# A chunked state-space scan: the old state's product scaled after the matmul, and three elementwise steps moved to GpSimd

## The chip, the core and the metric

The kernel runs on one core of one Trainium2 chip. The metric is the device time of one execution in microseconds (us). A core has five engines that run beside each other: PE (TensorE, matrix products into PSUM), DVE (VectorE), ACT (ScalarE), POOL (GpSimd) and SP (SyncE, which here issues all DMAs). Each takes its instructions in a fixed order that is settled when the program is built; they wait for each other by semaphores.

## The reference

One block of 2048 tokens by 1024 channels goes through a Mamba-2 layer, then through an attention layer with a sliding window. The change lies in the scan of the Mamba-2 layer, in chunks of 128 tokens, with 4 groups of 8 heads of 64 channels and a state of 128 per head. Cut to that:

```python
a_cum = jnp.cumsum(dt * a.reshape(SSM_GROUPS, SSM_HPG), axis=2)
xdt = x * dt[..., None]
seg = a_cum[:, :, :, None] - a_cum[:, :, None, :]
decay = jnp.exp(jnp.where(causal, seg, -jnp.inf))
cb = jnp.einsum('bcign,bcjgn->bcijg', cm, bm)
y_diag = jnp.einsum('bcijg,bcijgr,bcjgrp->bcigrp', cb, decay, xdt)
decay_to_end = jnp.exp(a_cum[:, :, -1:] - a_cum)
states = jnp.einsum('bcjgn,bcjgr,bcjgrp->bcgrpn', bm, decay_to_end, xdt)
chunk_decay = jnp.exp(a_cum[:, :, -1])
...
    return carry * dec[..., None, None] + st, carry
...
y_off = jnp.einsum('bcign,bcgrpn,bcigr->bcigrp', cm, prev, jnp.exp(a_cum))
return (y_diag + y_off).reshape(b, s, SSM_HEADS, SSM_HEAD_DIM)
...
y = y + d_skip.astype(jnp.float32)[:, None] * xs.astype(jnp.float32)
```

After it y is gated by SiLU(z), normed over each group and projected back.

## The kernel before

The tokens are cut into 4 blocks of 512, each block into 4 groups of channels: 16 units. For unit n the kernel computes ten products of the block's input with weight tiles (`gemm_steps`, L444 on): six go through a causal convolution (`conv`: B, C and four tiles of x), four become the gate (`zz`). One such product is 24 PE instructions at L163 into a PSUM tile `g` (two of them exist). The weights come by DMA (`ws`), ACT makes a rounded copy and DVE the remainder (L112, L113), two products ahead of their use.

While unit n's products run, the scan of unit n-1 runs beside them (`ssd_steps`). The list `SSD` gives the order of its steps, which are laid between the products' steps; on top of that the compiler's scheduler orders each engine's instructions. A unit has 4 chunks c, each with two halves hf of 4 heads:

- `l` (`load`, L547): a DMA broadcasts a row of the cumulated decays (`acd`) to `ab`, one per half.
- `p` (`prep`, L526): PE transposes x to `xt` and B to `bc`, and multiplies B by C; DVE makes `xdt` (L538) and `xw` (L540), `cbm` (L544).
- `h` (`half`, L552): ACT makes `ea` = exp(ab) (L557) and `seg` (L561, L562), DVE multiplies `ea` by C (L563) and `seg` by `cbm` (L564).
- `r` (`prod`, L567): PE adds in `y` the chunk's own part (L576, from `seg`) and the old state's part (L580: weights `prev`, moving `ea`).
- `f` (`fin`, L582): PE makes the chunk's own state `st` (L587), DVE multiplies the state `prev` by the chunk's decay (L589) and adds `st` (L590); DVE adds the skip term to y (four L593, into `yt`) and gates (two L597); ACT squares into `q` (L598); POOL adds the squares into `gacc` (L599, L602).
- `s` (`gn_sum`): PE transposes `gacc` to `rb` (L98), from which the group's norm comes.

In three units (the third group of blocks 0 to 2) the input norm of the next block is taken as well: ACT squares eight tiles (`sq`, L281), POOL adds them into `sqa` (L282). The convolution keeps its three last columns in `carry`, copied by POOL (L468, L474).

All of this is f32. `xt`, `bc`, `y`, `st` and `g` lie in PSUM, the other tiles named here in SBUF. PSUM is full: `y`, `xt`, `bc`, `st` one bank each, two for `rb` and two for `g`. The tail of the program, from about 1300 us, is the attention layer; the change leaves the order of its instructions as it is.

Of the kernel before, what the change touches and what calls it, by code (L numbers as in the profile page):

```python
# [9 lines left out]
F32 = mybir.dt.float32  # L10
F32R = mybir.dt.float32r
I32 = mybir.dt.int32
AF = mybir.ActivationFunctionType
ALU = mybir.AluOpType
# [43 lines left out]
def trunk(ctx: ExitStack, tc: tile.TileContext, xT, pT, pos, wts, wdt, vec, out):  # L58
    nc = tc.nc
# [12 lines left out]
    def vc(name, i=0, n=1):  # L72
        o = _V[name][0] + i
        return VA[0][:, o : o + n] if o < NVA else V[:, o - NVA : o - NVA + n]
# [226 lines left out]
    with ExitStack() as sa:  # L301
        sp = sa.enter_context(tc.tile_pool(name="sa", bufs=2))
        one = sa.enter_context(tc.tile_pool(name="oa", bufs=1))
        tp = sa.enter_context(tc.tile_pool(name="ta", bufs=2))
        pa = sa.enter_context(tc.tile_pool(name="paa", bufs=1, space=PSUM))
# [29 lines left out]
        prev = one.tile([128, 4, 512], F32, name="prev")  # L335
# [62 lines left out]
        def dt_path(b, ps):  # L398
# [12 lines left out]
            t = lambda n: one.tile([128, 128], F32, tag=n, name=n)  # L411
# [23 lines left out]
            wend = one.tile([128, 128], F32, tag="wend", name=f"wend{b}", bufs=2)  # L435
            nc.vector.tensor_tensor(wend, pm[:, 128:256], ac, op=ALU.subtract)
            nc.scalar.activation(wend, wend, AF.Exp)
            nc.vector.tensor_tensor(wend, wend, dt, op=ALU.mult)
            cdec = one.tile([128, 128], F32, tag="cdec", name=f"cdec{b}", bufs=2)
            nc.scalar.activation(cdec, pm[:, 128:256], AF.Exp)  # L440
            at = one.tile([128, 128], F32, tag="at", name="at")
# [80 lines left out]
        def ssd_steps(n):  # L522
# [3 lines left out]
            st8 = {}  # L526

            def prep(c):
                cs = slice(c * 128, c * 128 + 128)
                col = slice(c * 32 + 8 * g, c * 32 + 8 * g + 8)  # L530
                xt = pa.tile([128, 8, 64], F32, tag="xt", name="xt")
                for t in range(4):
                    nc.tensor.transpose(xt[:, 2 * t : 2 * t + 2].rearrange("p a b -> p (a b)"), xbc[t // 2][:, t % 2, cs], ident)
                bc = pa.tile([128, 256], F32, tag="bc", name="bc")
                nc.tensor.transpose(bc[:, 0:128], xbc[2][:, 0, cs], ident)
                nc.tensor.matmul(bc[:, 128:256], xbc[2][:, 0, cs], xbc[2][:, 1, cs], start=True, stop=True)
                xdt = sp.tile([128, 8, 64], F32, tag="xdt", name="xdt")
                nc.vector.tensor_tensor(xdt, xt, dt[:, col].unsqueeze(2).broadcast_to((128, 8, 64)), op=ALU.mult)  # L538
                xw = sp.tile([128, 8, 64], F32, tag="xw", name="xw")
                nc.vector.tensor_tensor(xw, xt, wend[:, col].unsqueeze(2).broadcast_to((128, 8, 64)), op=ALU.mult)  # L540
                bt = sp.tile([128, 128], F32, tag="bt", name="bt")
                nc.scalar.copy(bt, bc[:, 0:128])
                cbm = sp.tile([128, 128], F32, tag="cbm", name="cbm")
                nc.vector.tensor_tensor(cbm, bc[:, 128:256], tri, op=ALU.mult)  # L544
                st8[c] = [xdt, xw, bt, cbm, None]

            def load(c, hf):  # L547
                ab = st8["ab", c, hf] = sp.tile([128, 4, 128], F32, tag="ab", name="ab")
                i = 8 * c + 2 * g + hf
                nc.sync.dma_start(ab.rearrange("p a b -> p (a b)"), acd[i : i + 1, :].broadcast_to((128, 512)))  # L550

            def half(c, hf):  # L552
                cs = slice(c * 128, c * 128 + 128)
                cbm = st8[c][3]
                ab = st8.pop(("ab", c, hf))
                ea = sp.tile([128, 4, 128], F32, tag="ea", name="ea")
                nc.scalar.activation(ea, ab, AF.Exp)  # L557
                seg = sp.tile([128, 4, 128], F32, tag="seg", name="seg")
                for h in range(4):
                    hc = c * 32 + 8 * g + 4 * hf + h  # L560
                    nc.scalar.activation(seg[:, h], ab[:, h], AF.Relu, scale=-1.0, bias=ac[:, hc : hc + 1])  # L561
                nc.scalar.activation(seg, seg, AF.Exp, scale=-1.0)  # L562
                nc.vector.tensor_tensor(ea, ea, xbc[2][:, 1, cs].unsqueeze(1).broadcast_to((128, 4, 128)), op=ALU.mult)  # L563
                nc.vector.tensor_tensor(seg, seg, cbm.unsqueeze(1).broadcast_to((128, 4, 128)), op=ALU.mult)  # L564
                st8[c, hf] = (ea, seg)

            def prod(c, hf):  # L567
                if hf == 0:
                    st8[c][4] = pa.tile([128, 4, 128], F32, tag="y", name="y")
                xdt, y = st8[c][0], st8[c][4]  # L570
                ea, seg = st8.pop((c, hf))
                for t in range(2):
                    for r in range(2):
                        h = 4 * hf + 2 * t + r
                        o = y[64 * r : 64 * r + 64, 2 * hf + t, :]
                        nc.tensor.matmul(o, xdt[:, h], seg[:, 2 * t + r], start=True, stop=False)  # L576
                    for r in range(2):
                        h = 4 * hf + 2 * t + r
                        o = y[64 * r : 64 * r + 64, 2 * hf + t, :]
                        nc.tensor.matmul(o, prev[:, g, 64 * h : 64 * h + 64], ea[:, 2 * t + r], start=False, stop=True)  # L580

            def fin(c):  # L582
                cs = slice(c * 128, c * 128 + 128)
                col = slice(c * 32 + 8 * g, c * 32 + 8 * g + 8)
                xdt, xw, bt, cbm, y = st8.pop(c)
                st = pa.tile([128, 512], F32, tag="st", name="st")
                nc.tensor.matmul(st, bt, xw.rearrange("p a b -> p (a b)"), start=True, stop=True)  # L587
                pv = prev[:, g].rearrange("p (a b) -> p a b", a=8)
                nc.vector.tensor_tensor(pv, pv, cdec[:, col].unsqueeze(2).broadcast_to((128, 8, 64)), op=ALU.mult)  # L589
                nc.vector.tensor_tensor(prev[:, g], st, prev[:, g], op=ALU.add)  # L590
                yt = sp.tile([128, 4, 128], F32, tag="yt", name="yt", bufs=1)
                for t in range(4):
                    nc.vector.scalar_tensor_tensor(yt[:, t], xbc[t // 2][:, t % 2, cs], vc("dsk", 4 * g + t), y[:, t],  # L593
                                                   op0=ALU.mult, op1=ALU.add)
                q = sp.tile([128, 4, 128], F32, tag="q", name="q", bufs=1)
                for t in range(2):
                    nc.vector.tensor_tensor(sz[t][:, :, cs], yt[:, 2 * t : 2 * t + 2], sz[t][:, :, cs], op=ALU.mult)  # L597
                    nc.scalar.activation(q[:, 2 * t : 2 * t + 2], sz[t][:, :, cs], AF.Square)  # L598
                nc.gpsimd.tensor_tensor(q[:, 0:2], q[:, 0:2], q[:, 2:4], op=ALU.add)  # L599
                if c == 0:  # L600
                    st8["acc"] = tp.tile([128, T], F32, tag="gacc", name="gacc", bufs=1)
                nc.gpsimd.tensor_tensor(st8["acc"][:, cs], q[:, 0], q[:, 1], op=ALU.add)  # L602
# [535 lines left out]
```

## Time and profile before

| | us |
|---|---|
| median of 3 runs | 2926.93 (2926.82 to 2929.85) |
| the profiled execution | 2929.66 |
| its span, first to last instruction | 2927.8 |
| PE busy | 2883.9 (98%) |
| DVE busy | 2242.7 (77%) |
| ACT busy | 1633.8 (56%) |
| POOL busy | 379.9 (13%) |
| DMA, mean busy share of 16 engines | 34% |

How to read it. Busy time is the union of an engine's instructions; PE's ends are modelled, so a busy PE need not be at its peak. PEld is PE's loading of weights, which overlaps its products. The table by stretches gives for each stretch its length, then busy us (and number of instructions) of PE, PEld, DVE, ACT and POOL, then the granted clock as a share of 2.4 GHz, the DMA share and GB/s. The list of waits gives who waited for whom: us in total, times, the longest. Groups of instructions read: line, engine, operation, out<-in, shapes, count | busy us, mean ns of one | idle time of the engine before them and who ended it. For one line or tile: the count, then the shortest, median and longest in ns, then the first and last start in us. In a timeline each row is: start us, us, engine, line, operation, out<-in, shapes, how many in a row, and in brackets the idle time before and what ended it. DMA issues give the count, KB each and the median us to landing. L12 is line 12 of the kernel of before.

### The profile page before, as it was taken

The page shows a single profiled execution, that of the slowest core. Times are in us where ns is not written, and L with a number is a line of the kernel's source. Part 1 is how long each engine was busy: PE and PEld are TensorE (multiplying, and loading weights), DVE is VectorE, ACT ScalarE, POOL GpSimd, SP SyncE. Part 2 cuts the span into 40 slices and gives each one's busy share as a digit, 9 for nine tenths or more (in the row PEclk, how much of TensorE's full clock was granted, in tenths as well). Part 3 has the DMA queues.
Part 4 walks back from the last instruction along what each step waited for, and adds up shares of the span by engine and source line. Part 5 has one row for each costly group of instructions (what it writes and reads, how often), then busy time and mean ns, then how long its engine had stood idle before and what let it go on. Part 6 is the DMA issues. An engine that isn't in the chain of part 4 may idle for free.

```text
span 2927.8 us, 41254 instructions
## 1 busy us (share of the span) xinstructions
PE 2883.9 (98%) x14648; PEld 2250.0 (77%) x14648; DVE 2242.7 (77%) x4919; ACT 1633.8 (56%) x3309; POOL 379.9 (13%) x439
## 2 busy tenths in 40 slices
PE   8999999999999999999999999999999999999999
PEld 6777777777777777778777888777888768887667
DVE  7999989998899888766786646876556876557864
ACT  5666666666666666544665334674335764345752
POOL 1121113111311111111001011001010001010001
PEclk9999999999999999999999999999999999999999
DMA  4433433343333333533123532124422124432112
GB/s 161 137 109 117 137 120 107 114 138 126 105 119 113 116 119 121 172 110 95 59 74 113 176 95 90 54 97 134 147 94 83 57 94 138 144 94 89 51 62 82
DMA packets 134125, 319.43 MB, mean 109 GB/s; under 512 B 21152, under 2 KB 46624, under 8 KB 132896
## 3 DMA queue, kind: packets, MB, share of 16 engines
q1 hardware_dynamic: 133920, 316.80, 33.5%
q8 instruction: 115, 1.88, 0.3%
q14 instruction: 90, 0.74, 0.1%
HBM read 290.80 MB, written 25.95 MB: 108 GB/s over the span
## 4 chain that ended last, share of the span: by engine, by line
PE 50%; DVE 2%; ACT 1%; DMA 1%; issue 0%; SPq 0%; POOL 0%; ACTq 0%; POOLq 0%
PE g L163 12%; PE o L163 8%; PE tk L787 7%; PE gt L163 6%; PE ao L163 6%; PE pv L867 4%; PE pp L163 3%; PE pt L863 2%; PE sc L830 1%; PE sc L831 1%; PE qtp L979 1%; DMA raw<-ydr 0%; PE ktp L956 0%; DMA ws<-in_wts 0%; DVE w L146 0%; ACT P L847 0%
## 5 line engine op out<-in xcount | busy, mean ns | idle before, releaser
L163 PE MATMUL g<-u,w 128*128 128x512 f32 x5136 | 1239.4, 395 | 1.2 <-DVE x L492 0.7
L163 PEld LDWEIGHTS g<-u,w 128*128 128x128 f32 x5136 | 953.3, 188 | 220.2 <-issue 21.6
L112 ACT ACTIVATE w<-ws 128x1024 fp32r<-128x1024 f32 x336 | 355.3, 1058 | 410.1 <-PE g L163 137.9
L113 DVE TENSOR_TENSOR w<-ws,w 128x1024 fp32r<-128x1024 f32 x336 | 418.5, 1246 | 93.4 <-ACT w L112 92.8
L282 POOL TENSOR_TENSOR sqa<-sqa,sq 128x512 f32<-128x512 f32 x105 | 161.0, 1533 | 1482.2 <-ACT sq L281 1481.3
L163 PE MATMUL o<-y,w 128*128 128x512 f32 x1248 | 295.9, 392 | 4.1 <-ACT y L112 4.1
L787 PE MATMUL tk<-w,u 128*128 128x512 f32 x1152 | 291.2, 397 | 0.0
L163 PEld LDWEIGHTS o<-y,w 128*128 128x128 f32 x1248 | 232.9, 188 | 57.3 <-ACT y L112 6.8
L787 PEld LDWEIGHTS tk<-w,u 128*128 128x128 f32 x1152 | 210.4, 188 | 42.2 <-issue 3.2
L479 DVE SCALAR_TENSOR_TENSOR acc<-raw,cw,acc 128x512 f32<-128x512 f32 x288 | 219.9, 765 | 4.6 <-ACT acc L477 4.6
L163 PE MATMUL ao<-o,w 128*128 128x512 f32 x768 | 195.0, 397 | 2.5 <-DVE h L991 2.5
L163 PE MATMUL gt<-u,w 128*128 128x512 f32 x768 | 184.1, 394 | 4.3 <-ACT hsq L797 4.3
L561 ACT ACTIVATE seg<-ab,ac 128x128 f32<-128x128 f32 x512 | 166.6, 392 | 24.0 <-PE y L576 24.0
L145 ACT ACTIVATE w<-ws,V 128x256 fp32r<-128x256 f32 (+1 forms) x224 | 123.2, 597 | 93.9 <-issue 33.0
L146 DVE SCALAR_TENSOR_TENSOR w<-ws,V,w 128x256 fp32r<-128x256 f32 (+1 forms) x224 | 126.5, 595 | 63.0 <-ACT w L145 62.4
L163 PEld LDWEIGHTS gt<-u,w 128*128 128x128 f32 x768 | 141.3, 188 | 34.4 <-ACT hsq L797 6.0
L847 ACT ACTIVATE P<-P,nm,r 128x256 f32<-128x256 f32 x256 | 150.7, 591 | 28.9 <-DVE nm L841 28.9
L163 PEld LDWEIGHTS ao<-o,w 128*128 128x128 f32 x768 | 139.5, 188 | 33.8 <-issue 9.4
L599 POOL TENSOR_TENSOR q<-q 128x256 f32<-128x256 f32 x64 | 77.4, 1210 | 372.0 <-ACT q L598 372.0
L473 ACT COPY raw<-g 128x512 f32<-128x512 f32 x90 | 52.6, 585 | 127.6 <-PE g L163 126.5
L481 ACT ACTIVATE th<-acc 128x512 f32<-128x512 f32 x96 | 60.5, 631 | 101.7 <-DVE acc L479 101.7
L867 PE MATMUL pv<-pt,VV 128*64 128x512 f32 x256 | 113.9, 618 | 0.7
(231 smaller groups left out, 4352.9 us busy)
## 6 DMA issues: line engine op xcount, KB each, us to landing
ws<-in_wts SPq DMA_DIRECT2D x368, 512.0 KB, 3.5
ab<-acd SPq DMA_DIRECT2D x128, 256.0 KB, 3.4
ws<-in_wts SPq DMA_DIRECT2D x96, 256.0 KB, 2.9
ydr<-x SPq DMA_DIRECT2D x32, 512.0 KB, 2.6
raw<-ydr SPq DMA_DIRECT2D x48, 256.0 KB, 4.3
x<-in_xT SPq DMA_DIRECT2D x32, 256.0 KB, 5.2
h<-in_xT SPq DMA_DIRECT2D x8, 1024.0 KB, 6.0
out_h<-h SPq DMA_DIRECT2D x32, 256.0 KB, 2.8
```

The costliest lines, as they stand in the source:

```text
L112: nc.scalar.activation(hi, src, AF.Copy)
L113: nc.vector.tensor_tensor(lo, src, hi.bitcast(F32), op=ALU.subtract)
L145: nc.scalar.activation(w[:, 0, sl], raw[:, sl], AF.Copy, scale=sc)
L146: nc.vector.scalar_tensor_tensor(w[:, 1, sl], raw[:, sl], sc, w[:, 0, sl].bitcast(F32), op0=ALU.mult, op1=ALU.subtract)
L163: nc.tensor.matmul(ps, w[:, p, kw, cols], act[ka][:, q], start=first and j == 0 and r == 0, stop=last and j == n - 1 and r == 2)
L282: self.eng.tensor_tensor(self.acc, self.acc, q, op=ALU.add)
L479: nc.vector.scalar_tensor_tensor(acc, raw[:, j : j + T], tap(j), acc, op0=ALU.mult, op1=ALU.add)
L561: nc.scalar.activation(seg[:, h], ab[:, h], AF.Relu, scale=-1.0, bias=ac[:, hc : hc + 1])
L599: nc.gpsimd.tensor_tensor(q[:, 0:2], q[:, 0:2], q[:, 2:4], op=ALU.add)
L787: nc.tensor.matmul(res[s], a[k][:, x, s * 128 : s * 128 + 128], w[:, y, k % 2], start=k == 0 and j == 0, stop=k == 7 and j == 2)
L847: nc.scalar.activation(P[:, h], P[:, h], AF.Exp, scale=r8[:, h : h + 1], bias=nm[:, h : h + 1], accum_out=den[:, h : h + 1])
L867: nc.tensor.matmul(pv[64 * r : 64 * r + 64, :], VV[:, s + kh, 64 * a : 64 * a + 64], pts[r][:, kh], start=kh == 0, stop=kh == 1)
```

## The change

The old state's part of y is no longer made from `ea` times C. PE multiplies `prev` by C directly, for all 8 heads in four products of 128 weight columns, into a PSUM tile `off` (which shares its bank with `st`); DVE multiplies `off` by exp(a_cum), which a DMA now lays out by channel in a tile `ea` of its own; POOL adds the result to `yt`. POOL also does `xw` (now from `xdt`), the skip products (into `yt`, already in `prep`) and the state's decay. DVE then adds y to `yt` in one instruction. The core of the diff:

```diff
-            nc.vector.tensor_tensor(wend, wend, dt, op=ALU.mult)
...
-                nc.vector.tensor_tensor(xw, xt, wend[:, col].unsqueeze(2).broadcast_to((128, 8, 64)), op=ALU.mult)
+                nc.gpsimd.tensor_tensor(xw, xdt, wend[:, col].unsqueeze(2).broadcast_to((128, 8, 64)), op=ALU.mult)
...
+                yt = sp.tile([128, 4, 128], F32, tag="yt", name="yt")
+                for t in range(2):
+                    nc.gpsimd.tensor_tensor(yt[:, 2 * t : 2 * t + 2], xbc[t][:, :, cs],
+                                            vc("dsk", 4 * g + 2 * t, 2).unsqueeze(2).broadcast_to((128, 2, 128)), op=ALU.mult)
...
+                if hf == 0:
+
+                    ea = st8["ea", c] = sp.tile([128, 4, 128], F32, tag="ea", name="ea")
+                    rows = acd.rearrange("a (t r i) -> (a t) r i", t=2, r=2)
+                    for r in range(2):
+                        nc.sync.dma_start(ea[64 * r : 64 * r + 64],
+                                          rows[2 * i : 2 * i + 4, r].unsqueeze(0).broadcast_to((64, 4, 128)))
...
-                ea = sp.tile([128, 4, 128], F32, tag="ea", name="ea")
-                nc.scalar.activation(ea, ab, AF.Exp)
+                if hf == 0:
+                    nc.scalar.activation(st8["ea", c], st8["ea", c], AF.Exp)
...
-                nc.vector.tensor_tensor(ea, ea, xbc[2][:, 1, cs].unsqueeze(1).broadcast_to((128, 4, 128)), op=ALU.mult)
...
+                    off, ea, yt = pa.tile([128, 4, 128], F32, tag="st", name="off"), st8.pop(("ea", c)), st8[c][5]
+                    for t in range(4):
+                        nc.tensor.matmul(off[:, t], prev[:, g, 128 * t : 128 * t + 128], xbc[2][:, 1, cs], start=True, stop=True)
+                    nc.vector.tensor_tensor(ea, off, ea, op=ALU.mult)
+                    nc.gpsimd.tensor_tensor(yt, yt, ea, op=ALU.add)
...
-                        nc.tensor.matmul(o, xdt[:, h], seg[:, 2 * t + r], start=True, stop=False)
-                    for r in range(2):
-                        h = 4 * hf + 2 * t + r
-                        o = y[64 * r : 64 * r + 64, 2 * hf + t, :]
-                        nc.tensor.matmul(o, prev[:, g, 64 * h : 64 * h + 64], ea[:, 2 * t + r], start=False, stop=True)
+                        nc.tensor.matmul(o, xdt[:, h], seg[:, 2 * t + r], start=True, stop=True)
...
-                nc.vector.tensor_tensor(pv, pv, cdec[:, col].unsqueeze(2).broadcast_to((128, 8, 64)), op=ALU.mult)
+                nc.gpsimd.tensor_tensor(pv, pv, cdec[:, col].unsqueeze(2).broadcast_to((128, 8, 64)), op=ALU.mult)
...
-                yt = sp.tile([128, 4, 128], F32, tag="yt", name="yt", bufs=1)
-                for t in range(4):
-                    nc.vector.scalar_tensor_tensor(yt[:, t], xbc[t // 2][:, t % 2, cs], vc("dsk", 4 * g + t), y[:, t],
-                                                   op0=ALU.mult, op1=ALU.add)
+                nc.vector.tensor_tensor(yt, yt, y, op=ALU.add)
```

The change also moves instructions on the engines. In the changed kernel `xw` is L539, the skip products L546, `ea`'s DMAs L559, its exp L567, `off` L586, off times ea L587, the yt add L588, y's own part L593, `st` L600, the state's decay L602, its sum L603, yt plus y L604, the gating L607, ACT's squares L608, q and gacc L609 and L612; the other lines differ from before by one to ten.

POOL in a unit with the next block's norm, before: the carry copies, the sums of the squares (`sqa`) and of the gated output (`q`, `gacc`).

```order
L474 COPY carry<-raw 128x3
L468 COPY raw<-carry 128x3
L282 TENSOR_TENSOR sqa<-sqa,sq 128x512 x2
L599 TENSOR_TENSOR q<-q 128x256
L602 TENSOR_TENSOR gacc<-q 128x128
L282 TENSOR_TENSOR sqa<-sqa,sq 128x512 x4
L474 COPY carry<-raw 128x3
L282 TENSOR_TENSOR sqa<-sqa,sq 128x512
```

The same place in the changed kernel, from the state's decay of the unit's second chunk on:

```order
L602 TENSOR_TENSOR prev<-prev,cdec_2971 128x512
L467 COPY raw<-carry 128x3
L546 TENSOR_TENSOR yt<-x_0_3669,VA 128x256
L546 TENSOR_TENSOR yt<-x_1_3670,VA 128x256
L539 TENSOR_TENSOR xw<-xdt,wend_2968 128x512
L609 TENSOR_TENSOR q<-q 128x256
L282 TENSOR_TENSOR sqa<-sqa,sq 128x512
L612 TENSOR_TENSOR gacc<-q 128x128
L282 TENSOR_TENSOR sqa<-sqa,sq 128x512 x2
L588 TENSOR_TENSOR yt<-yt,ea 128x512
L282 TENSOR_TENSOR sqa<-sqa,sq 128x512 x4
L473 COPY carry<-raw 128x3
```

Ahead of the series stand four of the moved instructions and within it a fifth; the carry copy now comes after the last sum.

ACT at that place, before: the squares for the norm (`sq`) and for the output (`q`), and the copy of a product's PSUM tile `g` to `raw`, after which L477 frees it.

```order
L281 ACTIVATE sq<-x_4751 128x512 x2
L598 ACTIVATE q<-x_3_3738 128x256
L598 ACTIVATE q<-x_4_3739 128x256
L281 ACTIVATE sq<-x_4751 128x512 x2
L557 ACTIVATE ea<-ab 128x512
L281 ACTIVATE sq<-x_4751 128x512 x2
L473 COPY raw<-g 128x512
L281 ACTIVATE sq<-x_4751 128x512
L477 ACTIVATE acc<-g,cw 128x512
```

And in the changed kernel:

```order
L608 ACTIVATE q<-x_4_3673 128x256
L281 ACTIVATE sq<-x_4672 128x512 x2
L571 ACTIVATE seg<-ab,ac_2966 128x128
L281 ACTIVATE sq<-x_4672 128x512 x2
L571 ACTIVATE seg<-ab,ac_2966 128x128
L281 ACTIVATE sq<-x_4672 128x512
L571 ACTIVATE seg<-ab,ac_2966 128x128
L281 ACTIVATE sq<-x_4672 128x512 x2
L472 COPY raw<-g 128x512
L476 ACTIVATE acc<-g,cw 128x512
```

The copy moved from ahead of the last square to behind it, and parts of the next `seg` stand between the squares.

DVE at the end of an ordinary unit, before: the last chunk's state, skip term and gating, up to the reduction of `rb` (L100), which follows PE's transposes of `gacc`.

```order
L492 SCALAR_TENSOR_TENSOR x_4_3739<-th,g 128x512
L113 TENSOR_TENSOR w_4397<-ws_4395,w_4397 128x1024
L589 TENSOR_TENSOR prev<-prev,cdec_3021 128x512
L593 SCALAR_TENSOR_TENSOR yt<-x_0_2957,VA,y 128x128
L590 TENSOR_TENSOR prev<-st,prev 128x512
L593 SCALAR_TENSOR_TENSOR yt<-x_0_2957,VA,y 128x128
L593 SCALAR_TENSOR_TENSOR yt<-x_1_2958,VA,y 128x128 x2
L597 TENSOR_TENSOR x_3_2960<-yt,x_3_2960 128x2x128
L597 TENSOR_TENSOR x_4_2961<-yt,x_4_2961 128x2x128
```

And in the changed kernel:

```order
L491 SCALAR_TENSOR_TENSOR x_4_4370<-th,g 128x512
L587 TENSOR_TENSOR ea<-off,ea 128x512
L113 TENSOR_TENSOR w_5044<-ws_5042,w_5044 128x1024
L603 TENSOR_TENSOR prev<-st,prev 128x512
L604 TENSOR_TENSOR yt<-yt,y 128x512
L607 TENSOR_TENSOR x_3_3672<-yt,x_3_3672 128x2x128
L607 TENSOR_TENSOR x_4_3673<-yt,x_4_3673 128x2x128
L100 TENSOR_REDUCE rmsx<-rb 128x4
```

Five instructions left this stretch of DVE and two came; between off times ea (L587) and yt plus y (L604) lies POOL's yt add, during which DVE has a weight remainder (L113).

## Rows read from the trace of the kernel before

**Rows 1.** Busy times by stretches, the scan's stretch.

```profile
100.00:1240.00 1140.00, 1128.68 (x6460) 884.13 (x6459) 1025.43 (x1913) 720.17 (x1490) 231.08 (x318) 1.00 0.37 122
```

**Rows 2.** Waits of PE over the whole run.

```profile
PE y L576 <- DVE seg L564: 4.3, 3, 1.4
PE rb L98 <- POOL gacc L602: 4.2, 6, 1.0
```

**Rows 3.** Timeline of PE, from 240 to 242 us.

```profile
240.40 0.39 PE L536 MATMUL bc<-x 128*128 128x128 f32 x2
240.62 0.60 PE L98 MATMUL rb<-ident,sqa 128*128 128x128 f32 x4
...
241.42 0.39 PE L580 MATMUL y<-ea,prev 128*64 128x128 f32 x4
241.64 0.39 PE L576 MATMUL y<-seg,xdt 128*64 128x128 f32 x4
```

**Rows 4.** Groups of instructions, DVE and ACT, whole run.

```profile
L563 DVE TENSOR_TENSOR ea<-ea,x 128x512 f32<-128x512 f32 x128 | 90.4, 714 | 0.0
...
L557 ACT ACTIVATE ea<-ab 128x512 f32<-128x512 f32 x128 | 79.7, 623 | 3.9 <-DMA ab<-acd 2.9 <-PE y L580 0.5 <-DMA ydr<-x 0.4
...
L593 DVE SCALAR_TENSOR_TENSOR yt<-x,VA,y 128x128 f32<-128x128 f32 x256 | 77.2, 340 | 0.0
...
L589 DVE TENSOR_TENSOR prev<-prev,cdec 128x512 f32<-128x512 f32 x64 | 48.8, 763 | 6.0 <-PE y L580 5.3
...
L590 DVE TENSOR_TENSOR prev<-st,prev 128x512 f32<-128x512 f32 x64 | 43.7, 682 | 0.2 <-issue 0.2
...
L540 DVE TENSOR_TENSOR xw<-xt,wend 128x512 f32<-128x512 f32 x64 | 43.5, 680 | 0.0
```

**Rows 5.** POOL's instructions at L282 and at L599: shortest, median, longest.

```profile
L282 POOL TENSOR_TENSOR sqa<-sqa,sq x105: 1271/1362/2159, 184.8 to 2868.7; 128x512 f32<-128x512 f32 x105
...
L599 POOL TENSOR_TENSOR q<-q x64: 726/936/2308, 114.8 to 1270.3; 128x256 f32<-128x256 f32 x64
```

**Rows 6.** DVE's instructions at L597, L593 and L113: shortest, median, longest.

```profile
L597 DVE TENSOR_TENSOR x<-yt,x x128: 407/418/1518, 113.5 to 1269.3; 128x256 f32<-128x256 f32 x128
...
L593 DVE SCALAR_TENSOR_TENSOR yt<-x,VA,y x256: 329/340/348, 111.0 to 1268.7; 128x128 f32<-128x128 f32 x128
...
L113 DVE TENSOR_TENSOR w<-ws,w x336: 1195/1221/2285, 11.1 to 2902.7; 128x1024 fp32r<-128x1024 f32 x168
```

**Rows 7.** Busy times by stretches, a series of sqa.

```profile
184.80:197.40 12.60, 11.17 (x69) 8.48 (x69) 11.71 (x12) 6.43 (x13) 11.39 (x9) 1.00 0.13 43
```

**Rows 8.** Timeline of all engines in that stretch.

```profile
184.84 2.95 DVE L597 TENSOR_TENSOR x<-yt,x 128x256 f32<-128x256 f32 x2
...
190.57 2.29 DVE L113 TENSOR_TENSOR w<-ws,w 128x1024 fp32r<-128x1024 f32 x1
...
190.79 0.44 PE L576 MATMUL y<-seg,xdt 128*64 128x128 f32 x4 [1.43 <-DVE seg L564]
...
191.80 0.63 ACT L281 ACTIVATE sq<-x 128x512 f32<-128x512 f32 x1 [2.00 <-POOL sqa L282]
...
191.82 5.74 PE L163 MATMUL g<-u,w 128*128 128x512 f32 x24
192.78 1.77 DVE L563 TENSOR_TENSOR ea<-ea,x 128x512 f32<-128x512 f32 x1
...
194.48 1.78 DVE L589 TENSOR_TENSOR prev<-prev,cdec 128x512 f32<-128x512 f32 x1
```

**Rows 9.** Groups of POOL between 100 and 1240 us.

```profile
L282 POOL TENSOR_TENSOR sqa<-sqa,sq 128x512 f32<-128x512 f32 x21 | 33.1, 1576 | 3.8 <-ACT sq L281 2.9
```

**Rows 10.** Timeline at the end of an ordinary unit.

```profile
450.38 0.47 POOL L602 TENSOR_TENSOR gacc<-q 128x128 f32<-128x128 f32 x1
...
450.94 0.60 PE L98 MATMUL rb<-ident,gacc 128*128 128x128 f32 x4
```

**Rows 11.** DMA issues: the row of ab.

```profile
ab<-acd SPq DMA_DIRECT2D x128, 256.0 KB, 3.4
```

More of the change, by code (lines that the diff above doesn't have):

```diff
@@ L544, in prep @@
                 nc.vector.tensor_tensor(cbm, bc[:, 128:256], tri, op=ALU.mult)
-                st8[c] = [xdt, xw, bt, cbm, None]
+                yt = sp.tile([128, 4, 128], F32, tag="yt", name="yt")
+                for t in range(2):
+                    nc.gpsimd.tensor_tensor(yt[:, 2 * t : 2 * t + 2], xbc[t][:, :, cs],
+                                            vc("dsk", 4 * g + 2 * t, 2).unsqueeze(2).broadcast_to((128, 2, 128)), op=ALU.mult)
+                st8[c] = [xdt, xw, bt, cbm, None, yt]
             def load(c, hf):
@@ L562, in half @@
                 nc.scalar.activation(seg, seg, AF.Exp, scale=-1.0)
-                nc.vector.tensor_tensor(ea, ea, xbc[2][:, 1, cs].unsqueeze(1).broadcast_to((128, 4, 128)), op=ALU.mult)
                 nc.vector.tensor_tensor(seg, seg, cbm.unsqueeze(1).broadcast_to((128, 4, 128)), op=ALU.mult)
-                st8[c, hf] = (ea, seg)
+                st8[c, hf] = seg
             def prod(c, hf):
@@ L570, in prod @@
                 xdt, y = st8[c][0], st8[c][4]
-                ea, seg = st8.pop((c, hf))
+                seg = st8.pop((c, hf))
+                if hf == 0:
+                    cs = slice(c * 128, c * 128 + 128)
+                    off, ea, yt = pa.tile([128, 4, 128], F32, tag="st", name="off"), st8.pop(("ea", c)), st8[c][5]
[3 more added lines that the diff above has]
+                    nc.gpsimd.tensor_tensor(yt, yt, ea, op=ALU.add)
                 for t in range(2):
@@ L584, in fin @@
                 col = slice(c * 32 + 8 * g, c * 32 + 8 * g + 8)
-                xdt, xw, bt, cbm, y = st8.pop(c)
+                xdt, xw, bt, cbm, y, yt = st8.pop(c)
                 st = pa.tile([128, 512], F32, tag="st", name="st")
```

## The prediction

> **What bounds the kernel now.** I read the busy times of the scan's stretch first, then the waits of PE, then lines and single instructions. Between 100 and 1240 us PE is busy 1128.7 of 1140 us, at a granted clock of 1.00, its 2.4 GHz level [rows 1]. So at most 11.3 us of PE's idle time can be won there, 0.4% of the run, unless PE's own work gets shorter. DVE is second with 1025.4 us (90%), POOL has 231 us [rows 1]. What PE waits for by name is small: 4.3 us for seg from DVE and 4.2 us for gacc from POOL, over the whole run [rows 2]. The reader is to see that DVE at 90% sits beside a PE at 99%: work taken from DVE is taken from an engine on which PE hardly waits.
>
> **PE.** The 512 products of prev with ea (1024 instructions of 64 weight columns) become 256 products off with 128 columns (512 instructions). They look halved, but are not: two 64-column instructions run side by side on the two halves of the array. Four L580 start at 241.42 and the next four instructions at 241.64, 55 ns each; two full-width L536 start at 240.40 and the next at 240.62, 110 ns each [rows 3]. So 1024 x 0.055 = 56 us go and 512 x 0.110 = 56 us come. Below, nothing lets off run faster than L536. Above, 10% for eight full-width weight loads in a row, an estimate: 6 us more. I take +1 us.
>
> **DVE and ACT.** Gone from DVE: ea times C 90.4, xw 43.5, the state's decay 48.8, the skip term 77.2 us: 259.9 us [rows 4]. New on DVE: off times ea and yt plus y, 64 each. Both have one input in PSUM, as L590 has, 683 ns [rows 4]: 87.4 us. Net 172.5 us off DVE. ACT loses half of L557, 39.9 us [rows 4]; it waits on others most of the time there (720 of 1140 us busy [rows 1]), so I cost it at nothing; its cover is the PE products it runs beside.
>
> **POOL.** It gains five instructions in each of 64 chunks: xw, the state's decay and yt plus ea at 512 columns, two skip products at 256. The nearest rows are sqa, 1.27 us at best, and q, 0.73 at best [rows 5]: 64 x (3 x 1.27 + 2 x 0.73) = 337 us. With its 231 us that is about half of the stretch. POOL is not full, but its work runs into DVE's. When POOL works, a DVE instruction with both inputs in SBUF stretches: L597 goes from 418 to 1518 ns and L113 from 1221 to 2285, while L593, with an input in PSUM, never exceeds 348 [rows 6]. POOL stretches too: q from 0.73 to 2.31 us [rows 5].
>
> How much DVE loses is the disputed price. One stretch shows it: from 184.8 to 197.4 us POOL is busy 11.39 us [rows 7]. There two L597 take 2.95 instead of 0.84 us; L113 takes 2.29 instead of 1.22; L563 takes 1.77 and L589 1.78, where their groups average 0.71 and 0.76 [rows 4, 6, 8]. That is 2.1 + 1.1 + 1.1 + 1.0 = 5.3 us, 0.47 us of DVE for each us of POOL. The 337 us would then cost DVE 158 us: of the 172.5 us taken off it, 14 stay off. The lower end is none lost, since a POOL instruction can fall into DVE's idle time; the upper end is all 337. I take 0.47, the row in which POOL runs as densely as it now will. DVE stays near 90%.
>
> The Trainium skill ("SBUF — State Buffer", Who interferes with whom) states the stronger rule: a DVE instruction with two SBUF inputs and a GpSimd instruction that reads SBUF exclude each other for the whole instruction, and the second fully blocks. By it the sum would take the upper end, the second rival; the stretch above shows half of that.
>
> **What becomes late.** In PE's order the next chunk's off mostly comes 5 us or more behind st, so the decay on POOL (which waits only for off of its own chunk) has room, and xw is wanted some 20 us after it can start (estimates from the pitch of single instructions [rows 3, 8]). Two places have no room.
>
> First, the three units in which the next block's norm is summed (sqa). POOL's order there puts a decay, two skip products, xw and a yt add into the series of squares, and ACT's copy of a gemm's PSUM tile now stands behind all squares, where before it stood ahead of the last. ACT already stood still 2.0 us there for one sqa [rows 8]. From off of the second chunk to the square that frees the copy POOL does eight 512-column instructions at the stage's mean of 1.58 us [rows 9], three of 256 at 0.94 (q's median [rows 5]), gacc 0.47 [rows 10] and a small copy 0.2: 16.1 us. Three ACT instructions of 0.62 (L557's mean [rows 4]) follow: 18.0. PE comes back for that bank after 23 gemm instructions, a half y, st, 24 gemm instructions, xt and bc. A gemm's 24 take 5.6 us (5.74 with the last one's end [rows 8]), the small ones about 2.1 us at 0.11 us per 128 columns [rows 3]: 13.1 us. PE waits 4.9 us, three times: +14.7 us. The 1.43 us that it waits for seg at this spot in each of the three units [rows 2, 8] are swallowed: -4.3 us. Between none (POOL finds the gaps) and 9 us per unit, this term is the widest.
>
> Second, each unit's end. The last gacc ends 0.1 us before PE starts the transposes on it: 450.38 + 0.47 against 450.94 [rows 10]. Now the chain is off, decay and yt add on POOL, yt plus y and the gating on DVE, ACT, q, gacc. Four L593 and the decay leave DVE there (1.4 and 0.8 us [rows 4]); yt plus y (0.7) and the yt add (1.27) enter, so the bare chain is as long as before, 2.0 against 2.2. But the add now meets DVE's L113 (1.22 us [rows 6]) on the way; I count a third of it, 0.4, less the 0.2: 0.2 us later in each of 15 units, +3 us, between -4.2 (all of PE's wait gone [rows 2]) and +15 (the whole L113 each time, less the 0.2).
>
> **SP and the queues.** 128 more DMAs, each half of ab, which lands in 3.4 us [rows 11]. They are issued one or two chunks ahead, but wait for POOL to free ea; the weight loads queue behind them on SP. A gemm's weights are split two gemms ahead, some 11 us, so this is covered unless POOL falls behind by more than that.
>
> Sum: +1 + 14.7 - 4.3 + 3 = +14.4 us on the profiled execution's 2929.7, 2944.1. That execution lies 2.7 above the median of the runs, 2926.9, so the time to compare is 2941.4 us, 0.5% slower.
>
> **Rivals.** (a) Faster. DVE is relieved after all, because POOL's instructions fall into DVE's idle time and its PSUM inputs; the waits at both places stay as they are and PE's idle time in the stretch goes: at best 2926.9 - 11.3 = 2916, likelier 2919 (both named waits gone, 8.5 us [rows 2]). For it: 115 us of the stretch have DVE idle [rows 1]. Against: all that PE could win is 11 us, and POOL now stands in two chains that it did not stand in. It decides if DVE loses under 0.2 us per us of POOL.
> (b) The port fills. By the rule above each us of POOL costs DVE one: 1025 - 172 + 337 = 1190 us of DVE in a stretch of 1140, 50 us too much: 2977. For it: L597 at 1518 ns waited for nearly a whole sqa [rows 6]. Against: 0.47 in the one dense stretch. It decides from about 0.85 us per us.
> (c) No change: POOL keeps up in the three units, PE's waits trade places, within 6 us of 2927.
>
> **How the numbers follow.** About 0.2%, 5.9 us, is what a measurement of this kernel can tell from no change. Chances: forecast (2931 to 2955) 0.46, (a) 0.17, (b) and what lies toward it 0.14, (c) 0.23. The lower end of the range is (a)'s likelier value, 2919, the upper (b)'s, 2977; some 2 in 10 lie outside. Faster 0.17 is (a). Slower is (b) and the forecast less its near edge, 0.55. The rest, 0.28, is no change.
>
> **What would show it.** Right: between 100 and 1240 us PE's off group takes as long as y from ea did; POOL is busy about 600 us or more; DVE stays above 85%, with L113, L478 and L573 stretched; PE waits some us for ACT's copy in the three units with sqa. Wrong: DVE below 80% busy with its two-input instructions near their medians (rival a); DVE at 98% and PE waiting for seg and weights in every unit (rival b); off groups at another pitch than 0.11 us; PE waits in units without sqa.

## The result and the profile after

The changed kernel takes 3023.4 us (median of 4 runs, 3020.2 to 3026.4) against 2928.0 for the kernel before: a ratio of 1.032, 95% interval 1.031 to 1.033. It is slower by 95 us, where 14 were forecast and 50 were the worst that the range allowed for. The profiled execution has a span of 3024.6 us against 2927.8.

The page of the kernel after, busy time of each engine (share of the span, number of instructions):

```profile
PE 2913.0 (96%) x14136; PEld 2272.6 (75%) x14136; DVE 2198.2 (73%) x4531; ACT 1600.9 (53%) x3245; POOL 755.1 (25%) x759
```

PE was busy for 2883.9 us before and is now busy for 2913.0, though it has fewer instructions; its idle time rose from 43.9 to 111.6 us. So of the 96.8 us of span some 68 are standing and 29 are slower work. DVE lost 44.5 us of work instead of the 14 that were forecast: it was not the engine that got in the way. The scan's stretch says the same, in the columns of [rows 1] (window, length, busy time of PE, PEld, DVE, ACT, POOL, granted clock, DMA share, GB/s):

```profile
100.00:1240.00 1140.00, 1069.03 (x5509) 838.53 (x5508) 910.66 (x1433) 636.37 (x1322) 552.81 (x589) 0.97 0.40 123
```

All engines but POOL are less busy than before, DVE at 80% instead of 90%, and the clock is 0.97 instead of 1.00. (The same work now ends later, so the stretch holds a little less of it.) When every engine has time and the end is later, look for a chain that passes through several of them. The waits of the kernel after, whole run (engine, line, what it waited for: us in all, times, longest):

```profile
ACT ea L567 <- DMA ea<-acd: 125.0, 34, 8.8
...
DVE seg L573 <- ACT seg L572: 61.3, 15, 6.5
```

The waits of PE alone, the same columns, against [rows 2]:

```profile
PE y L593 <- DVE seg L573: 44.1, 12, 5.9
PE g L163 <- ACT acc L476: 10.1, 3, 3.4
PE rb L98 <- POOL gacc L612: 7.0, 4, 1.9
...
PE off L586 <- DVE prev L603: 5.2, 8, 0.9
```

And SP's, whose only work is to issue DMAs in order, between 60 and 1340 us:

```profile
SPq L559 <- POOL yt L588: 361.9, 59, 13.1
SPq L136 <- DVE w L113: 248.4, 86, 17.7
SPq L553 <- ACT seg L571: 130.4, 38, 8.9
```

Read upward, this is one chain. PE waits for seg, seg's last step on DVE waits for ACT, ACT stands before the exponential of ea until ea's DMA has landed, and SP has held that DMA back until POOL's add (L588) has read what was in the buffer. One link of it in the timeline of all engines, around 145 us:

```profile
138.84 1.74 POOL L588 TENSOR_TENSOR yt<-yt,ea 128x512 f32<-128x512 f32 x1
...
140.60 0.58 SPq L559 DMA_DIRECT2D ea<-acd  x1
...
141.28 0.55 SPq L136 DMA_DIRECT2D ws<-in_wts  x1
141.93 0.37 SPq L553 DMA_DIRECT2D ab<-acd  x1
142.36 0.58 SPq L559 DMA_DIRECT2D ea<-acd  x1
143.03 0.55 SPq L553 DMA_DIRECT2D ab<-acd  x1
...
148.98 0.63 ACT L567 ACTIVATE ea<-ea 128x512 f32<-128x512 f32 x1 [8.77 <-DMA ea<-acd]
149.52 0.70 ACT L608 ACTIVATE q<-x 128x256 f32<-128x256 f32 x2
150.13 0.61 ACT L572 ACTIVATE seg<-seg 128x512 f32<-128x512 f32 x1
...
150.77 0.86 DVE L573 TENSOR_TENSOR seg<-seg,cbm 128x512 f32<-128x512 f32 x1 [6.47 <-ACT seg L572]
...
151.69 1.12 PE L593 MATMUL y<-seg,xdt 128*64 128x128 f32 x8 [5.89 <-DVE seg L573]
```

POOL's add ends at 140.58 and SP issues at once, five DMAs within 3 us, with weights between the two halves of ea. ACT stands for 8.77 us, and the ready seg of the running chunk stands behind it. The exponential is not even wanted yet: the ea made at 148.98 is multiplied at 182.29. It is the same in the whole scan: ACT stands for over 3 us before L567 15 times, and the 12 stands of 4.5 us or more are each followed within 3 us by one of PE's 12 waits for seg, the three shorter ones (up to 3.8 us) by none. What this does to PE stands in the windows of 2 us after it:

```profile
144.00:146.00 2.00, 1.80 (x18) 1.40 (x16) 0.30 (x1) 0.00 (x0) 1.34 (x2) 1.00 0.95 216
146.00:148.00 2.00, 0.00 (x0) 0.00 (x0) 0.00 (x0) 0.00 (x0) 0.00 (x0) 1.00 0.92 316
148.00:150.00 2.00, 0.00 (x0) 0.00 (x0) 0.00 (x0) 1.02 (x3) 0.00 (x0) 1.00 0.33 127
150.00:152.00 2.00, 0.31 (x4) 0.31 (x6) 1.23 (x2) 2.00 (x4) 1.56 (x3) 0.54 0.01 4
152.00:154.00 2.00, 2.00 (x10) 1.24 (x7) 2.00 (x3) 2.00 (x7) 2.00 (x2) 0.50 0.00 0
154.00:156.00 2.00, 2.00 (x5) 1.11 (x4) 0.69 (x3) 1.65 (x5) 1.16 (x1) 0.50 0.00 0
156.00:158.00 2.00, 2.00 (x8) 1.61 (x7) 1.40 (x4) 0.73 (x2) 0.49 (x1) 0.76 0.55 125
158.00:160.00 2.00, 2.00 (x10) 1.65 (x9) 0.00 (x0) 0.00 (x0) 1.85 (x4) 1.00 0.99 348
```

PE stands for 5.9 us, and from shortly before its end to about 157 us the granted clock is 0.50, the 1.2 GHz level. So the wait is paid for once more in part: some 5 us at half speed cost about 2.6 us on top (an estimate from these windows).

### The profile page after: what moved, and what is told of

It is laid out like the page before. It is cut to its first block, busy times and chain, and to the rows that moved or that the text cites. A ratio compares the mean times of both kernels' runs of the same rounds, so it can differ in the third digit from the quotient of the medians.

```text
span 3024.6 us, 40439 instructions
## 1 busy us (share of the span) xinstructions
PE 2913.0 (96%) x14136; PEld 2272.6 (75%) x14136; DVE 2198.2 (73%) x4531; ACT 1600.9 (53%) x3245; POOL 755.1 (25%) x759
## 4 chain that ended last, share of the span: by engine, by line
PE 53%; DVE 4%; ACT 2%; DMA 1%; POOL 1%; issue 1%; SPq 0%; ACTq 0%; POOLq 0%; DVEq 0%
PE g L163 12%; PE o L163 10%; PE tk L797 7%; PE gt L163 6%; PE ao L163 5%; PE pv L877 4%; PE pp L163 3%; PE pt L873 2%; PE sc L840 1%; PE sc L841 1%; DVE acc L478 1%; PE qtp L989 1%; DMA ea<-acd 1%; DMA raw<-ydr 0%; DVE w L113 0%
## 5 line engine op out<-in xcount | busy, mean ns | idle before, releaser
L163 PE MATMUL g<-u,w 128*128 128x512 f32 x5136 | 1258.8, 399 | 10.4 <-ACT acc L476 10.1
L282 POOL TENSOR_TENSOR sqa<-sqa,sq 128x512 f32<-128x512 f32 x105 | 154.9, 1475 | 1471.6 <-ACT sq L281 1470.6
L113 DVE TENSOR_TENSOR w<-ws,w 128x1024 fp32r<-128x1024 f32 x336 | 448.3, 1335 | 89.9 <-ACT w L112 89.1
L478 DVE SCALAR_TENSOR_TENSOR acc<-raw,cw,acc 128x512 f32<-128x512 f32 x288 | 251.6, 875 | 42.7 <-ACT acc L476 42.7
L163 PEld LDWEIGHTS ao<-o,w 128*128 128x128 f32 x768 | 139.5, 188 | 33.8 <-issue 9.4
L573 DVE TENSOR_TENSOR seg<-seg,cbm 128x512 f32<-128x512 f32 x128 | 118.1, 923 | 61.6 <-ACT seg L572 61.3
L546 POOL TENSOR_TENSOR yt<-x,VA 128x256 f32<-128x256 f32 x128 | 114.3, 912 | 103.9 <-DVE x L607 100.3
L593 PE MATMUL y<-seg,xdt 128*64 128x128 f32 x1024 | 87.1, 295 | 45.1 <-DVE seg L573 44.1
```

What stands on the lines that cost most here:

```text
L113: nc.vector.tensor_tensor(lo, src, hi.bitcast(F32), op=ALU.subtract)
L163: nc.tensor.matmul(ps, w[:, p, kw, cols], act[ka][:, q], start=first and j == 0 and r == 0, stop=last and j == n - 1 and r == 2)
L282: self.eng.tensor_tensor(self.acc, self.acc, q, op=ALU.add)
L478: nc.vector.scalar_tensor_tensor(acc, raw[:, j : j + T], tap(j), acc, op0=ALU.mult, op1=ALU.add)
```

## The experiments

Medians, and the ratio to the kernel before on the same chip (2930.2 to 2930.6 us in these series) with its 95% interval. The kernel after was measured beside a kernel before of 2928.0, so a difference to its 3023.4 us is uncertain by some 3 us:

| run | edit | us | ratio |
|---|---|---|---|
| e1_ea3 | third buffer for ea | 3032.4 | 1.035 (1.033 to 1.037) |
| e2_yt3 | third buffer for yt | 3030.0 | 1.035 (1.033 to 1.036) |
| e3_add_dve | the add on DVE | 2954.2 | 1.008 (1.007 to 1.010) |
| e4_all_dve | all five steps on DVE | 2939.7 | 1.003 (1.002 to 1.004) |
| e6_eo | product in a tile of its own | 2963.7 | 1.012 (1.010 to 1.013) |
| e7_eb | load in a tile of its own | 2956.4 | 1.009 (1.007 to 1.010) |
| e8_add_only | only the add on POOL | 2965.6 | 1.012 (1.010 to 1.013) |
| e9_before_xw_decay | before, xw and decay on POOL | 2938.3 | 1.003 (1.002 to 1.004) |
| e10_eb_eo | both tiles | 2954.7 | 1.008 (1.007 to 1.010) |
| e11_eb_sqdve | e7, squares' sums on DVE | 2938.4 | 1.003 (1.002 to 1.004) |
| e12_before_sqdve | before, squares' sums on DVE | 2927.4 | 0.999 (0.998 to 1.000) |
| e13_before_xw_decay_sqdve | e9 and e12 together | 2930.0 | 1.000 (0.999 to 1.001) |

**e1: a third buffer for ea.**

```diff
-  ea = st8["ea", c] = sp.tile([128, 4, 128], F32, tag="ea", name="ea")
+  ea = st8["ea", c] = sp.tile([128, 4, 128], F32, tag="ea", name="ea", bufs=3)
```

> The changed kernel with a third buffer for ea; the order of PE and DVE stays as it is. Theory T (ea's buffer): the DMA of ea waits on SP until POOL's add into yt has read the old ea (361.9 us of SP's waits in the changed kernel), so ea lands late, ACT stands 125.0 us before the exponential of ea, seg comes late, PE stands (44.1 us at y) and then runs at the lower clock for a while. Then here SP waits under 60 us for POOL, ACT under 30 us for ea's DMA, PE under 12 us for seg, and the time is 2938 to 2968 us. Rival R (DVE and POOL hold each other up): the DVE work and its order are the same, so seg is as late as before and the time stays at 3010 to 3030 us. Rival S (off shares st's PSUM bank, and PE loses there): 3005 to 3030 us, with PE's wait for seg gone and one for prev in its place.

Theory T missed by 64 us, and the time is just above the ranges of R and S. The waits, SP's first and ACT's after it, are those of the kernel after to within 4 us:

```profile
SPq L559 <- POOL yt L588: 358.6, 58, 13.1
```

```profile
ACT ea L567 <- DMA ea<-acd: 121.7, 38, 8.1
```

The reason is in the trace of this run: the exponential for the fifth chunk starts at 124.90 us instead of 148.98, while its product is scaled at 180.01 against 182.29. The load and the exponential moved one chunk forward in their engines' orders, into the room that the buffer gave, and wait for the add of a chunk that is just as recent. Here the scheduler put the load as early as its buffers allowed, and one more buffer bought no slack. So this run did not test T: the wait that it was to remove stayed.

**e2: a third buffer for yt.**

```diff
-  yt = sp.tile([128, 4, 128], F32, tag="yt", name="yt")
+  yt = sp.tile([128, 4, 128], F32, tag="yt", name="yt", bufs=3)
```

> The changed kernel with a third buffer for yt and two for ea; the order of PE, DVE, ACT and SP stays, POOL's moves in places. The skip products stand 100.3 us on POOL until gating has freed yt, with xw, the decay and the add behind them. If that block is what makes POOL's add, and with it ea's DMA, late (theory T with its root at yt): POOL waits under 30 us for gating, SP's 361.9 us for POOL fall by a third or more, 2945 to 2995 us. If POOL is late by its own load and by DVE (R), or if the buffer of ea is held too long whatever POOL does: SP's wait falls by under a third, 3000 to 3030 us.

3030.0 us, and SP still waits 358.7 us for the add. That looks like the second reading, but the block that the run was to remove is still there: POOL's wait for gating was to fall under 30 us, and it was 100.3 in the kernel after. Here it is:

```profile
POOL yt L546 <- DVE x L607: 97.9, 38, 3.9
```

As with ea, the skip products moved one chunk forward into the new buffer (those of the third chunk start at 68.92 us instead of 112.65) and wait for an equally recent reader. Whether POOL's standing there makes the add late is left open by this run.

**e3: the add on DVE, and e4: all five steps on DVE.**

```diff
-  nc.gpsimd.tensor_tensor(yt, yt, ea, op=ALU.add)
+  nc.vector.tensor_tensor(yt, yt, ea, op=ALU.add)
```

> The changed kernel with the add of ea into yt on DVE, which frees ea right behind the product that made it; POOL keeps decay, xw and skip products. T: SP's wait for ea's reader falls below 100 us, ACT's for ea's DMA below 40 us, 2935 to 2975 us, though DVE has 64 more instructions with two SBUF inputs (some 50 us). R: DVE gains what POOL loses, 3005 to 3035 us.

> The changed kernel with all of POOL's new work (xw, decay, skip products, add) on DVE; off and its scaling at the product's output stay, and so does the load of ea by DMA. T and R both put it near the kernel before: 2925 to 2960 us, with DVE some 20 us above its 1025 us. S (the form of the product itself costs, or its PSUM bank): 2975 us or more. If the load of ea by DMA costs by itself, whoever frees the buffer: ACT still stands over 60 us for it and the time is over 2965 us.

One instruction per chunk, moved to DVE, gives 69 of the 93 us between the kernel after and the kernel before of this series (3023.4 to 2954.2, beside 2930.6). SP's wait for the freed ea is 52.8 us, ACT's for its DMA 21.2, PE's for seg 2.8. With all five steps on DVE (e4), 9 us are left, far from S's 2975, so S falls too: the product's new form and its bank cost little.

**e6 and e7: the same work on the same engines, with the chain cut.**

```diff
-  nc.vector.tensor_tensor(ea, off, ea, op=ALU.mult)
-  nc.gpsimd.tensor_tensor(yt, yt, ea, op=ALU.add)
+  eo = sp.tile([128, 4, 128], F32, tag="eo", name="eo", bufs=1)
+  nc.vector.tensor_tensor(eo, off, ea, op=ALU.mult)
+  nc.gpsimd.tensor_tensor(yt, yt, eo, op=ALU.add)
```

```diff
-  ea = st8["ea", c] = sp.tile([128, 4, 128], F32, tag="ea", name="ea")
+  ea = st8["eb", c] = sp.tile([128, 4, 128], F32, tag="eb", name="eb", bufs=1)
...
-  nc.scalar.activation(st8["ea", c], st8["ea", c], AF.Exp)
+  st8["ea", c] = sp.tile([128, 4, 128], F32, tag="ea", name="ea")
+  nc.scalar.activation(st8["ea", c], st8.pop(("eb", c)), AF.Exp)
```

> The changed kernel with DVE's scaled product in a tile of its own (eo, one buffer), so that ea is free when DVE has read it and POOL's add is out of the chain that loads ea; every engine has the same work. Theory T2 (the third buffer only let the load and its exponential move one chunk forward on SP and ACT, so the wait on POOL's add stayed; the chain is POOL's add, ea's DMA, ACT's exponential, seg, PE): SP's wait for whoever frees ea falls from 361.9 below 120 us, ACT's for ea's DMA from 125 below 50, PE's for seg from 44 below 15 us, with POOL as busy as in the changed kernel (over 520 of 1140 us): 2945 to 2980 us. Rival R (POOL's load and its clash with DVE make DVE and POOL late): 3005 to 3035 us.

> The changed kernel with the load into a tile of its own (eb, one buffer) and the exponential out of place into ea: the DMA now waits for ACT's last exponential, not for POOL, but the exponential itself still waits for POOL's add, which frees ea. T2: the DMA's landing (3 to 6 us) and the queue on SP leave the chain, POOL's add stays in it: between the changed kernel and the one with a tile for the product, 2950 to 3000 us, ACT's wait for ea under POOL's name. If SP's queue is what hurts (ws and ab stuck behind the load of ea): as good as with a tile for the product, within 10 us. R: 3005 to 3035 us.

2963.7 and 2956.4 us: 60 and 67 us come back without an instruction less on POOL, which is busy 761.0 and 758.6 us in the whole run, against 755.1 in the kernel after. PE, DVE and POOL take the same instructions in nearly the same order. So R falls, and the chain is shown. ACT's waits in the two runs, e6 first:

```profile
ACT ea L567 <- DMA ea<-acd: 116.4, 39, 4.5
```

```profile
ACT ea L568 <- POOL yt L589: 109.6, 41, 4.5
```

ACT stands nearly as long in all as in the kernel after (125.0), where under 50 us was expected of e6 (and SP waits 135.1 us for DVE's product, where under 120 was), but never over 4.5 us instead of 8.8; PE's wait for seg is 4.4 us in e6 and 0.7 in e7. A sum of waits says little here: in the kernel after each of PE's 12 waits is shorter by 1.7 to 3.2 us than the stand of ACT ahead of it, so PE has room for some 3 us, not for 8.8. In e7 SP no longer waits for POOL at L559 (its longest wait there is 7.7 us, and for ACT). DMAs still leave in bunches, but fewer: from 60 to 1340 us an issue is followed by four or more others within 3 us 17 times, against 36 in the kernel after. e7 is 7 us faster than e6 and not between it and the kernel after, as T2 had it; that is within what the other reading, SP's queue, allowed. How much of the loss is the late ea itself and how much the weights and ab that leave with it, the two runs do not separate: both free the load from POOL's add.

**e8: only the add on POOL** (xw, decay and skip products back on DVE, by the same replacement as in e3).

> The changed kernel with xw, the decay and the skip products on DVE; POOL keeps the add of ea into yt alone. T2 with POOL's lateness from its queue: the add comes right behind DVE's product, SP waits under 150 us for it, 2935 to 2970 us. If a hop over POOL in that chain is enough by itself, whatever else POOL does: 2980 us or more.

2965.6 us, near the upper end of T2's range, with POOL busy 373.7 us of the stretch. SP waits 236.4 us for the add, where under 150 was expected, the longest 14.7, and PE 10.9 us for seg. The hop over POOL in this chain costs some 26 us over e4 even where POOL has little else to do; the other 58 us up to the kernel after come only with xw, the decay and the skip products on POOL.

**e9: the kernel before with xw and decay on POOL.**

```diff
-  nc.vector.tensor_tensor(wend, wend, dt, op=ALU.mult)
...
-  nc.vector.tensor_tensor(xw, xt, wend[:, col].unsqueeze(2).broadcast_to((128, 8, 64)), op=ALU.mult)
+  nc.gpsimd.tensor_tensor(xw, xdt, wend[:, col].unsqueeze(2).broadcast_to((128, 8, 64)), op=ALU.mult)
...
-  nc.vector.tensor_tensor(pv, pv, cdec[:, col].unsqueeze(2).broadcast_to((128, 8, 64)), op=ALU.mult)
+  nc.gpsimd.tensor_tensor(pv, pv, cdec[:, col].unsqueeze(2).broadcast_to((128, 8, 64)), op=ALU.mult)
```

> The kernel before with xw (from xdt) and the decay on POOL, nothing else: the product with prev stays as it was and nothing is loaded into ea. T2: none of the changed kernel's 95 us is here, 2920 to 2950 us. R (two more POOL instructions of 512 columns in a chunk clash with DVE): 2955 us or more.

2938.3 us. Its page, busy time of each engine:

```profile
PE 2883.0 (98%) x14648; PEld 2251.4 (77%) x14648; DVE 2230.0 (76%) x4787; ACT 1638.3 (56%) x3309; POOL 580.7 (20%) x567
```

POOL gained 200.8 us over the kernel before. DVE gave up 92.3 us of its groups [rows 4] but is only 12.7 us less busy: it lost 79.6, or 0.40 us for each us of POOL, close to the price taken.

**e10 to e12: what is left.** e10 has both tiles of e6 and e7, one buffer each for eb, ea and eo. e11 is e7, and e12 the kernel before, with the sums of squares on DVE:

```diff
-  sq = Sq(tha, nc.vector if b == 0 else None)
+  sq = Sq(tha, nc.vector)
```

> Both decouplings at once: the load in eb, the exponential in ea, the product in eo, one buffer each; POOL's add then stands in no chain that leads to a load or an exponential. T2: ACT's 109.6 us before the exponential of ea (for POOL's add, in the kernel with eb alone) go, or turn into waits for DVE's product of under 60 us; PE waits for seg under 5 us; 2944 to 2958 us. If what is left over the kernel before has nothing to do with ea (the sums of squares, the unit ends, the product's form): within 5 us of 2956.

> The kernel with the load in a tile of its own (eb), and in it the sums of squares of the next block's norm (sqa) on DVE instead of POOL in the three units that have them. If POOL's series with xw, decay, skip and add in between is what makes PE wait for ACT's copy (10.1 us in three units): that wait falls under 3 us, and some of the waits at the end of the same units (8.4 us for gacc) go too: 2936 to 2949 us. If DVE is the one that is late there: 2950 to 2962 us.

> Control: the kernel before with the same sums of squares on DVE. Its waits for seg (4.3 us) and for gacc in those units (3 x 1.2) may go, DVE has some 5 us more in each: 2918 to 2931 us if POOL's squares caused them, 2930 to 2945 us if DVE, at 93% there, then becomes late. It tells how much of what the sums of squares give in the changed kernel is owed to the change.

e10 is at 2954.7: with ACT's 110 us of standing for POOL gone it is 1.7 us faster than e7, less than a measurement can tell, so that standing cost next to nothing, and what is left has little to do with ea. e11 is at 2938.4, 18 us under e7, and PE's wait for ACT's copy in the three units is gone. In the kernel before the same edit gives 2.8 us (e12), which a measurement can hardly tell from nothing. PE's waits in e11, whole run:

```profile
PE rb L98 <- POOL gacc L613: 7.6, 7, 1.8
PE dtps L394 <- ACT ux L116: 6.4, 3, 5.6
PE rb L107 <- DVE rmsy L90: 5.7, 4, 1.6
```

Its page and that of e7 say what the clock had cost: the same 14136 instructions of PE take 2913.0 us in the kernel after, 2889.3 in e7 and 2883.3 in e11, first e7:

```profile
PE 2889.3 (98%) x14136; PEld 2263.6 (77%) x14136; DVE 2178.9 (74%) x4531; ACT 1599.8 (54%) x3245; POOL 758.6 (26%) x759
```

```profile
PE 2883.3 (98%) x14136; PEld 2258.8 (77%) x14136; DVE 2200.3 (75%) x4552; ACT 1600.8 (55%) x3245; POOL 735.8 (25%) x738
```

The mean granted clock of the three runs is 0.989, 0.997 and 0.999. So some 24 us of PE's time went with the chain and 6 with the squares.

Where PE's time goes, summed from the traces: from the start of each instruction of PE to the start of the next one, put down to the first one's output tile, from the run's start to the first tk of the attention layer (us).

```
              before    after   e7_eb   e11_eb_sqdve
g              961.0    991.0   976.0      970.0
bc              19.8     30.3    29.0       18.2
off              0.0     62.9    62.3       62.3
y              131.4    128.8    77.2       78.3
st              51.9     46.9    42.2       42.1
the rest       187.7    188.6   190.5      189.1
sum           1351.8   1448.5  1377.2     1360.0
```

The sums differ by as much as the spans (96.7 of 96.8 us for the kernel after), so all of it lies ahead of the attention layer's tk. A wait is counted at the instruction ahead of it: the stalls for seg stand in y (128.8 against 77.2), the slow clock mostly in g, the wait for ACT's copy in bc.

**e13: the candidate for a faster version**, e9 and e12 together.

> The kernel before with xw and the decay on POOL and the sums of squares on DVE: the candidate for a version that beats both. With xw and decay on POOL alone it took 2938.3 us, the sums of squares on DVE alone gave 2927.4. If what POOL costs there comes from its series of squares, the two together are at 2922 to 2931 us. If xw and the decay cost at the units' ends (their kernel's waits for gacc are 8.7 us against 4.2 before), and only 3 us hang on the squares: 2933 to 2940 us.

2930.0 us, no change: most of the 8 us that xw and the decay cost on POOL in e9 hung on its squares (2.6 are left over e12), and without the squares they give nothing either. No run beats the kernel before by more than e12's 0.1%, which is within the 0.2% that a measurement of this kernel can tell.

## Why the prediction was wrong

The direction was right and the size was not: 2941.4 forecast, 2919 to 2977 as the range, 3023.4 measured. (The range's lower end was 2926.9 less the 8.5 us of waits, which is 2918 and not 2919.) Two of the signs that were named ahead spoke against the forecast: DVE fell to 80% of the stretch, under the 85% that it was to keep, and PE waited for seg in units without sqa too. Step by step:

- **SP and the queues: the step that failed.** "They are issued one or two chunks ahead, but wait for POOL to free ea ... so this is covered unless POOL falls behind by more than that." The wait was seen, and costed at nothing, because a gemm's 11 us of lead were counted for the weights. But the first victim is not the weights: it is the exponential of ea, which stands on ACT in order, ahead of the seg that PE wants next. The prediction costed ACT by its busy time (half of L557 gone) and never asked what is queued behind an ACT instruction that now waits for a DMA, where before it waited for nothing worth naming [rows 4]. Cutting this chain alone gives 67 us (e7), 70% of the loss. 11 us (e11 over e12) stay to the parts that were priced at 1 and 3, and 15 to the squares.
- **The clock was left out.** In the kernel before the granted clock of the stretch is 1.00 [rows 1], and no term had a price for its fall when PE stands for longer. Of the loss 29 us are PE's slower work; 24 of them go with the chain (PE is busy 2889.3 us in e7, for the same instructions) and so are part of its 67.
- **The three units with sqa: the mechanism was right, the size too small.** PE waits for ACT's copy in exactly those three units, 3.4 us each against 4.9, and the seg waits at that spot are gone, as said. This is the link, in the timeline of the kernel after:

```profile
203.81 1.29 POOL L588 TENSOR_TENSOR yt<-yt,ea 128x512 f32<-128x512 f32 x1
...
205.06 5.39 POOL L282 TENSOR_TENSOR sqa<-sqa,sq 128x512 f32<-128x512 f32 x4
...
205.13 0.69 DVE L604 TENSOR_TENSOR yt<-yt,y 128x512 f32<-128x512 f32 x1 [6.14 <-POOL yt L588]
...
207.78 0.63 ACT L281 ACTIVATE sq<-x 128x512 f32<-128x512 f32 x1 [0.78 <-POOL sqa L282]
208.31 0.57 ACT L472 COPY raw<-g 128x512 f32<-128x512 f32 x1
208.78 0.78 ACT L476 ACTIVATE acc<-g,cw 128x512 f32<-128x512 f32 x1
...
209.61 2.57 PE L163 MATMUL g<-u,w 128*128 128x512 f32 x10 [3.37 <-ACT acc L476]
```

  The series gives 18.0 us when it leaves POOL (e7 to e11); less the 2.8 that the squares cost in the kernel before, 15 against the +10.4 (14.7 less 4.3) of the sum. The waits were overpriced (10.1 us instead of 14.7); what the sum lacked is again the clock: PE's same instructions take 6.0 us less in e11 than in e7. DVE's 6.14 us behind the add, in the same series, was not foreseen.
- **Unit ends:** PE's wait for gacc went from 4.2 [rows 2] to 7.0 us, +2.8 against the +3 forecast. In e11 it is 7.6, and 5.7 us for rmsy come to it, which the kernel before has at 0.9: so a few us more than forecast.
- **PE's product:** off and y together take 139.5 us in e7 against 131.4, +8.1, where +1 was taken and 6 was the upper end; but st takes 9.7 less, of which 4.3 are the old waits for seg [rows 2]. Net some 3 us. The 110 ns of an off are as read: in e7 the median from one off to the next is 112 ns. From an off to a y it is 205, 55 times. That change to the pairs of 64 columns is not made more often than before (111 times in e7, 118 in the kernel before); there it mostly stood behind a g and was counted in that row, so some 5 of the 8.1 us only changed rows.
- **DVE and POOL:** POOL gained 375 us (337 forecast). Of the 172.5 us taken off DVE 44.5 stay off in the whole run: 128 lost, 0.34 us for each us of POOL, against 0.47 taken. Rival (b), the full port, came nearest in time and is wrong in mechanism: DVE is at 80%, and e11 with POOL nearly as busy (735.8 us) is 8 us from the kernel before. As the prediction read the rule of the Trainium skill behind it ("SBUF — State Buffer", Who interferes with whom), full blocking of the second one, POOL would have put 375 us on DVE; the 0.34 here and the 0.40 of e9 are under half of that. They are means over a whole run and do not speak against the rule for two single instructions that meet.
- **ACT costed at nothing because half idle:** it is busy 636 of 1140 us, less than before, and still the link that broke. Busy time was the wrong measure; what counts is the order in which it takes its instructions.

How the 11 us that stay in e11 over e12 split between the product's form and the late chains at the units' ends was read from the table and not tried by itself.

## What to carry to other kernels

When a change turns a computed tile into a loaded one, or lets another engine be its last reader, follow the buffer all the way round: who frees it, which queue waits for that, and what stands behind the instruction that needs it, on its own engine. An in-place chain (load, exponential, product, add in one tile) ties the load to its slowest last reader; a tile for the raw load cut 67 us here, while a third buffer of the same tile cut none. On a kernel whose PE is 99% busy, price a stall of several us with the time that follows at the lower clock, and look at the longest wait of a row before its sum.

## What was not expected of the hardware

- After standing for 5.9 us PE ran at 0.50 of its clock for some 5 us (151.7 to about 157 us in the kernel after). Over the run PE's same instructions took 23.7 us more than in e7, where its waits for seg are 0.7 us instead of 44.1: over half as much again as the waits.
- DMAs that SP had held back left together and filled the DMA engines: their share is 0.92 to 0.95 from 144 to 148 us and 0.00 to 0.01 from 150 to 156. A half of ea, which lands in 3.0 us in the median, took up to 6.5 in that kernel.
